# Accumulating transfers and row sums, read by nobody, inside a one-core transformer block; two weight staging tiles in place of three

## The chip, the cores and the metric

The program runs on one core of a Trainium2 chip. The metric is the device time of one execution in microseconds (us). Before the change it is 1162.78 us, the median of two runs (1161.66 and 1163.89).

## The reference

One block of a hybrid model over 512 tokens of width 1024, in float32. Three sublayers each normalise the tokens, scale and shift them by values computed from a conditioning vector `c`, and add their gated result back: a gated feed-forward layer, a mixer (pooling windows and a chunked state-space scan), and a second gated feed-forward layer; a last norm ends it.

```python
mod = (silu(c) @ w_ada + b_ada).reshape(bsz, 3, 3, 1024)      # shift, scale, gate of each sublayer
h = modulate(rmsnorm(x, norm_g[0]), shift[0], scale[0])
x = x + 0.5 * gate[0] * swiglu(h, ffn1_in, ffn1_out)           # swiglu: (silu(a) * b) @ w_out, width 2816
h = modulate(rmsnorm(x, norm_g[1]), shift[1], scale[1])
x = x + gate[1] * hybrid_mixer(h, ...)
h = modulate(rmsnorm(x, norm_g[2]), shift[2], scale[2])
x = x + 0.5 * gate[2] * swiglu(h, ffn2_in, ffn2_out)
return rmsnorm(x, final_g)
```

## The kernel before

Activations lie with the 1024 features on partitions (8 tiles of 128) and the 512 tokens along the row. Every product is made of three matmuls on split operands (`mm3`, L312 to L314): a number is split into a high part and the rest, and high x high, high x rest and rest x high are added in PSUM.

**Weights.** The class `Weights` streams them in units of up to eight 128x128 tiles. A unit is loaded by SyncE into a raw tile (`w_raw`, L103, 512 KB; there are `RAW` = 3 of them), cast to its high part on ScalarE (`w_hi`, L123), and the rest is taken on VectorE (`w_lo`, L126). High and rest stand in rings of `RING` = 5. A raw tile is free again when its unit's L126 is done, so the load of unit k waits for the split of unit k - 3. The first eight units (`w1s`, 384 KB each, 0 to 7) belong to the first stage, where six products of the first feed-forward layer are built over eight steps k while step k's modulation weights arrive as four 256 KB loads (`big<-in_ada_dram`, L395). From unit 8 on two units make one pair of the feed-forward layer.

**Feed-forward.** `ffn` goes over 22 pairs in portions of 8, 8 and 6. A pair is two products of 48 matmuls together; its gate product is a Silu on ScalarE, a multiplication on VectorE (L607), a cast on ScalarE (L325) and a difference on VectorE (L327). Pairs 0 to 2 come out of the first stage. After a portion, eight output columns are made from its pairs and added to `x` (L524).

**Modulation values.** In the first feed-forward layer a background generator, `ada_rest`, computes the remaining 14 half rows of modulation values: each is a sum on VectorE of eight steps (L464 for the first, L466 for seven more, each on a 256 KB tile loaded at L437), closed by four small matmuls on TensorE (L486, listed with their weight loads), a copy on ScalarE (L489) and four 0.5 KB transfers (L492). `pump` advances it six steps behind each pair. The matmuls for the second sum stand on TensorE behind pair 6, those for the third behind pair 7.

**What sets the order.** TensorE's order is the order in which the code is written. In the first stage (`start`) the other engines' order is as written too; behind it a scheduler orders ScalarE, VectorE, GpSimd and SyncE. Each engine executes its own list strictly in order, and SyncE's list holds all transfers. GpSimd has little: pieces of the norms, of pooling and of the scan.

Of the kernel before, what the change touches and what calls it, by code (L numbers as in the profile page):

```python
# [8 lines left out]
F32 = mybir.dt.float32  # L9
# [3 lines left out]
ALU = mybir.AluOpType  # L13
PSUM = bass.MemoryType.PSUM

P = 128
NT = 512
# [11 lines left out]
MLATE = 5  # L29
SPREAD1, SPREAD2, SPREAD3 = 3.6, 1.8, 2.4  # L30
RING = 5
RAW = 3
AHEAD = 3
NBIG = 50
NSQ = 2
# [49 lines left out]
class Weights:  # L85
# [13 lines left out]
    def load(self, upto):  # L99
        while len(self.raw) < min(upto, len(self.units)):  # L100
            ap, count, width, _ = self.units[len(self.raw)]
            raw = self.pool.tile([P, KD * P], F32, name="w_raw", tag="w_raw", bufs=RAW)
            self.nc.sync.dma_start(out=raw[:, :count * width], in_=ap)  # L103
# [26 lines left out]
    def fill(self, more=0):  # L130
# [5 lines left out]
        while len(self.split) < want and self.ring[len(self.split) + 1] - self.ring[used] <= RING:  # L136
            self.ensure(len(self.split) + 1)
        self.load(min(self.unit + AHEAD + RAW + more, len(self.split) + RAW))

# [98 lines left out]
class Block:  # L238
# [26 lines left out]
    def plan(self):  # L265
        a = self.a
        u = [(a["w1s"][k], 2 * NSTART, P, False) for k in range(KD)]

        def stream(ap):
            n = ap.shape[1] // P  # L270
            for t in range(0, n, KD):
                e = min(t + KD, n)
                u.append((ap[:, t * P:e * P], e - t, P, False))

        def ffn(f, first):
            for pi, (p0, p1) in enumerate(PORTIONS):
                for t in range(2 * max(p0, first), 2 * p1):
                    u.append((a["ffn%d_in" % f][t], KD, P, False))
                stream(a["ffn%d_out%d" % (f, pi)])

        def halves(ap):
            u.extend((ap[i], KD, P, True) for i in range(4))

        ffn(1, NSTART)
        halves(a["w_inH"])
        for kind, i in self.mixer_order():
            if kind == "in":
                u.append((a["w_in"][i], KD, P, False))
            elif kind != "dt" and i == 0:
                stream(a["w_out" + kind[3:]])  # L290
        halves(a["ffn2_inH"])
        ffn(2, 2)
        return u
# [323 lines left out]
    def ffn(self, h, gs, j, gate, norm, late, spread, pumps=(0, 0)):  # L617
        for pi, (p0, p1) in enumerate(PORTIONS):
            if pi:
                gs = {i: self.new_act() for i in range(p0, p1)}  # L620
            for i in range(max(p0, j), p1):
                self.pair(h, gs[i])
                self.pump(pumps[0])
            acts = [gs[i] for i in range(p0, p1)]
            last = pi == len(PORTIONS) - 1
            for m in range(late if last else KD):
                self.out_full(m, acts, gate, last)()
                self.pump(pumps[1])
            if last:
                self.pump(1000)  # L630
                norm = norm()
                for m in range(late):
                    norm.scale(m)
                self.out_halves(range(late, KD), acts, gate, norm, spread)


    def start(self):
# [549 lines left out]
```

## Time and profile before

| | |
|---|---|
| runs | 1161.66 and 1163.89 us, median 1162.78 |
| profiled execution | 1160.53 us, span 1158.5 us |
| TensorE busy | 1146.2 us, 99% of the span |
| VectorE busy | 629.9 us, 54% |
| ScalarE busy | 396.6 us, 34% |
| GpSimd busy | 119.3 us, 10% |
| transfers | 140.17 MB, all issued from SyncE |

The span is the time between the first and the last recorded instruction of the profiled execution; 2.0 us of its own time lie outside. Busy time is the sum of an engine's instructions; matmuls are pipelined, so a busy TensorE is not one at its peak. The chain that ended last is followed back from the last instruction to whatever released each step.

### The profile page before, as it was taken

The numbers are of one execution on the slowest core, as the hardware profiler recorded it, in microseconds if no ns is written. First come the engines' busy times: TensorE is split into PE (matmuls) and PEld (weight loads), VectorE is DVE, ScalarE is ACT, GpSimd is POOL, SyncE is SP. The second block draws the span as 40 slices with busy tenths as digits, with TensorE's granted clock in tenths as the row PEclk, the third lists the DMA queues.
The fourth block names the chain that finished last, engine by engine and source line by source line (L and its number), as shares of the span: only waits on it lengthen the run. The fifth ranks groups of instructions, "written<-read, shape, count | busy, mean of one in ns | idle before, by whom it ended". The sixth has DMA issues, their size and how long they took to land.

```text
span 1158.5 us, 15066 instructions
## 1 busy us (share of the span) xinstructions
PE 1146.2 (99%) x5948; PEld 940.8 (81%) x5948; DVE 629.9 (54%) x975; ACT 396.6 (34%) x660; POOL 119.3 (10%) x122
## 2 busy tenths in 40 slices
PE   8999999999999999999999999999999999999997
PEld 6677787777877997888888878899888888888887
DVE  4567736667363666677968595563333333333334
ACT  4352222221223453454544453343321222212232
POOL 0000000000000320023112561121000000000001
PEclk9999999999999999999999999999999999999999
DMA  9585735756352411222212213440332233323312
GB/s 346 170 293 178 261 115 198 256 190 228 123 178 91 141 60 52 77 73 73 74 55 73 73 56 91 124 131 20 91 91 91 93 103 96 92 91 91 95 33 73
DMA packets 52837, 140.17 MB, mean 121 GB/s; under 512 B 7456, under 2 KB 8864, under 8 KB 52768
## 3 DMA queue, kind: packets, MB, share of 16 engines
q1 hardware_dynamic: 52768, 139.23, 37.1%
q8 instruction: 46, 0.75, 0.3%
q14 instruction: 23, 0.19, 0.1%
HBM read 137.08 MB, written 2.10 MB: 120 GB/s over the span
## 4 chain that ended last, share of the span: by engine, by line
PE 98%; DVE 1%; DMA 0%; ACT 0%; SPq 0%; issue 0%; DVEq 0%; ACTq 0%
PE ps_mm L312 24%; PE ps_mm L313 23%; PE ps_mm L314 23%; PE ps_t L314 6%; PE ps_t L313 6%; PE ps_t L312 6%; PE ps_y L965 1%; PE ps_mm L352 1%; PE ps_mm L406 1%; PE ps_t L959 1%; PE ps_y L984 1%; PE ps_mm L375 1%; PE ps_t L927 0%; DMA x<-in_x_dram 0%; PE ps_t L930 0%; PE ps_t L932 0%
## 5 line engine op out<-in xcount | busy, mean ns | idle before, releaser
L312 PE MATMUL ps_mm<-big,w_hi 128*128 128x512 f32 (+1 forms) x1192 | 454.9, 382 | 0.0
L313 PE MATMUL ps_mm<-big,w_hi 128*128 128x512 f32 (+1 forms) x1192 | 448.1, 376 | 0.1
L314 PE MATMUL ps_mm<-big,w_lo 128*128 128x512 f32 (+1 forms) x1192 | 448.0, 376 | 0.0
L123 ACT CAST w_hi<-w_raw 128x1024 fp32r<-128x1024 f32 (+1 forms) x178 | 185.9, 1045 | 521.3 <-PE ps_mm L313 309.4
L126 DVE TENSOR_TENSOR w_lo<-w_raw,w_hi 128x1024 fp32r<-128x1024 f32 (+1 forms) x178 | 220.8, 1242 | 171.7 <-ACT w_hi L123 160.6
L312 PEld LDWEIGHTS ps_mm<-big,w_hi 128*128 128x128 f32 x1192 | 224.1, 188 | 50.3 <-issue 8.2
L314 PEld LDWEIGHTS ps_mm<-big,w_lo 128*128 128x128 f32 x1192 | 224.1, 188 | 44.8
L313 PEld LDWEIGHTS ps_mm<-big,w_hi 128*128 128x128 f32 x1192 | 224.2, 188 | 43.6 <-issue 0.7
L314 PE MATMUL ps_t<-big,w_lo 128*128 128x512 f32 x312 | 123.4, 396 | 0.0
L312 PE MATMUL ps_t<-big,w_hi 128*128 128x512 f32 x312 | 123.4, 396 | 0.0
L313 PE MATMUL ps_t<-big,w_hi 128*128 128x512 f32 x312 | 123.4, 396 | 0.0
L524 DVE SCALAR_TENSOR_TENSOR x<-ps_mm,mod,x 128x512 f32<-128x512 f32 (+1 forms) x79 | 51.1, 648 | 127.6 <-PE ps_mm L314 127.5
L331 POOL TENSOR_TENSOR sacc<-sacc,sq 128x256 f32<-128x256 f32 (+1 forms) x30 | 28.7, 956 | 747.4 <-ACT sq L386 416.1
L607 DVE TENSOR_TENSOR tmp<-tmp,ps_t 128x512 f32<-128x512 f32 x39 | 26.8, 688 | 104.4 <-PE ps_t L314 104.4
L466 DVE SCALAR_TENSOR_TENSOR big<-big,sc 128x512 f32<-128x512 f32 x98 | 73.6, 751 | 12.6 <-DMA big<-in_ada_dram 10.1
L314 PEld LDWEIGHTS ps_t<-big,w_lo 128*128 128x128 f32 x312 | 58.6, 188 | 14.2
L313 PEld LDWEIGHTS ps_t<-big,w_hi 128*128 128x128 f32 x312 | 58.6, 188 | 14.2
L312 PEld LDWEIGHTS ps_t<-big,w_hi 128*128 128x128 f32 x312 | 58.6, 188 | 14.1
L877 DVE SCALAR_TENSOR_TENSOR big<-ps_mm,vec,big 128x511 f32<-128x511 f32 (+2 forms) x60 | 44.7, 745 | 2.2 <-ACT big L875 1.3
L325 ACT CAST big<-tmp 128x512 fp32r<-128x512 f32 (+1 forms) x66 | 36.5, 556 | 2.0 <-DVE tmp L607 1.4
L312 PE MATMUL ps_mm<-big 128*128 128x256 f32 x128 | 36.5, 286 | 0.0
L313 PE MATMUL ps_mm<-big 128*128 128x256 f32 x128 | 36.2, 283 | 0.0
(179 smaller groups left out, 891.1 us busy)
## 6 DMA issues: line engine op xcount, KB each, us to landing
w_raw<-in_ffn_in_dram SPq DMA_DIRECT2D x78, 512.0 KB, 3.5
big<-in_ada_dram SPq DMA_DIRECT2D x144, 256.0 KB, 4.8
w_raw<-in_ffn_out_dram SPq DMA_DIRECT2D x44, 512.0 KB, 3.8
w_raw<-in_w_in_dram SPq DMA_DIRECT2D x32, 512.0 KB, 3.5
w_raw<-in_w_outB_dram SPq DMA_DIRECT2D x10, 512.0 KB, 3.6
w_raw<-in_w1s_dram SPq DMA_DIRECT2D x8, 384.0 KB, 5.8
w_raw<-in_w_outA_dram SPq DMA_DIRECT2D x6, 512.0 KB, 3.9
x<-in_x_dram SPq DMA_DIRECT2D x8, 256.0 KB, 5.3
```

The source lines that it names most:

```text
L123: nc.scalar.copy(out=hi[:, :n], in_=r)
L126: nc.vector.tensor_tensor(out=lo[:, :n], in0=r, in1=hi[:, :n].bitcast(F32), op=ALU.subtract)
L312: T.matmul(o, lhsT=hi, rhs=ahi[:, s], start=first, stop=False)
L313: T.matmul(o, lhsT=hi, rhs=alo[:, s], start=False, stop=False)
L314: T.matmul(o, lhsT=lo, rhs=ahi[:, s], start=False, stop=last)
L325: self.nc.scalar.copy(out=hi[:, s], in_=src[:, :n])
L331: self.nc.gpsimd.tensor_tensor(out=acc, in0=acc, in1=q, op=ALU.add)
L352: self.nc.tensor.matmul(ps[:, at + j:at + j + 1], lhsT=acc[:, c * P - c0:(c + 1) * P - c0], rhs=self.ones[:, 0:1], start=i == 0, stop=i == ...
L466: V.scalar_tensor_tensor(out=acc, in0=ws.pop(i), scalar=self.sc[:, q:q + 1], in1=acc, op0=ALU.mult, op1=ALU.add)
L524: self.nc.vector.scalar_tensor_tensor(out=xs, in0=ps[:, :n], scalar=self.mod[:, gate, m:m + 1], in1=xs, op0=ALU.mult, op1=ALU.add)
L607: nc.vector.tensor_tensor(out=g32, in0=sa, in1=pb[:, :n], op=ALU.mult)
L877: V.scalar_tensor_tensor(out=acc[:, s:], in0=ps[:, :NT - s], scalar=tap(3 - s), in1=acc[:, s:], op0=ALU.mult, op1=ALU.add)
```

## The change

A method `extra` is called in the second feed-forward layer behind pair 3. It takes two tiles of 128x2048 (t1, t2) and one of 128x512 (r), which nothing else reads. SyncE loads t1 and t2 from the weights `ffn2_out0`. GpSimd then issues 20 transfers that add into t2, eight over 1, 2, 4 and 4 pieces of 512 columns from memory and from t1, eight over 2 pieces each in four rounds, and four over one piece each. VectorE then makes three products with a row sum (L660), a copy, two scaled products with a row sum (L666), two additions over 2048 columns (L668, L669), a strided one (L671) and a small one (L672). The number of raw tiles goes from three to two, and the space reserved for GpSimd's transfer descriptors is set to 2048 bytes per partition.

```diff
-RAW = 3
+RAW = 2
...
             for i in range(max(p0, j), p1):
                 self.pair(h, gs[i])
+                if gate == 8 and i == 3:
+                    self.extra()
                 self.pump(pumps[0])
...
+    def extra(self):
+
+        nc = self.nc
+        G, V = nc.gpsimd, nc.vector
+        src = self.a["ffn2_out0"]
+        t1 = self.sb.tile([P, 4 * NT], F32, name="extra1")
+        t2 = self.sb.tile([P, 4 * NT], F32, name="extra2")
+        r = self.sb.tile([P, NT], F32, name="extra3")
+        nc.sync.dma_start(out=t1, in_=src[:, :4 * NT])
+        nc.sync.dma_start(out=t2, in_=src[:, 4 * NT:8 * NT])
+        for n in (1, 2, 4, 4):
+            G.dma_start(out=t2[:, :n * NT], in_=src[:, :n * NT], accum_op=ALU.add)
+        for n in (1, 2, 4, 4):
+            G.dma_start(out=t2[:, :n * NT], in_=t1[:, :n * NT], accum_op=ALU.add)
+        for _ in range(4):
+            for j in range(2):
+                c = slice(2 * j * NT, 2 * (j + 1) * NT)
+                G.dma_start(out=t2[:, c], in_=src[:, c], accum_op=ALU.add)
+        for j in range(4):
+            c = slice(j * NT, (j + 1) * NT)
+            G.dma_start(out=t2[:, c], in_=t1[:, c], accum_op=ALU.add)
+        for j in range(3):
+            V.tensor_tensor_reduce(out=t2[:, :2 * NT], in0=t2[:, :2 * NT], in1=t1[:, :2 * NT], scale=1.0,
+                                   scalar=r[:, 3:4] if j == 2 else 0.0, op0=ALU.mult, op1=ALU.add,
+                                   accum_out=r[:, j:j + 1] if j < 2 else r[:, 4:5])
+            if j == 1:
+                V.tensor_copy(out=r[:, 3:4], in_=r[:, 0:1])
+        for j in range(2):
+            V.scalar_tensor_tensor(out=t2[:, :2 * NT], in0=t2[:, :2 * NT], scalar=1.0, in1=t1[:, :2 * NT],
+                                   op0=ALU.mult, op1=ALU.mult, accum_out=r[:, 8 + j:9 + j])
+        V.tensor_tensor(out=t2, in0=t2, in1=t1, op=ALU.add)
+        V.tensor_tensor(out=t2, in0=t2, in1=t1, op=ALU.subtract)
+        a, b = (t.rearrange("p (s n) -> p s n", n=NT) for t in (t1, t2))
+        V.tensor_tensor(out=b[:, 1::2], in0=a[:, 0::2], in1=b[:, 3:4].broadcast_to([P, 2, NT]), op=ALU.add)
+        V.tensor_tensor(out=r, in0=t1[:, :NT], in1=t2[:, :NT], op=ALU.add)
...
-    nc = bacc.Bacc("TRN2", target_bir_lowering=False, num_devices=1)
+    nc = bacc.Bacc("TRN2", target_bir_lowering=False, num_devices=1, dynamic_dma_scratch_size=2048)
```

The scheduler does not keep the added work where the call stands. On SyncE, in the changed program, the loads of t1 (L646) and t2 (L647) stand in the first stage, t2's here between the modulation loads of step 6 and weight load 6; a DMAHW name is a semaphore of an earlier transfer, DVE one of VectorE (a split that frees a raw tile).

```order
L103 DMA w_raw_372<-in_w1s_dram 128x768 [waits DMAHW7_49,DVE_49]
L395 DMA big_417<-in_ada0_dram 128x512 [waits DMAHW0_49]
L395 DMA big_419<-in_ada0_dram 128x512 [waits DMAHW1_49]
L395 DMA big_421<-in_ada0_dram 128x512 [waits DMAHW2_49]
L395 DMA big_423<-in_ada0_dram 128x512 [waits DMAHW3_49]
L647 DMA extra2_7292<-in_ffn2_out0_dram 128x2048 [waits DMAHW4_49]
L103 DMA w_raw_425<-in_w1s_dram 128x768 [waits DMAHW5_49,DVE_49]
```

Before, the same queue has no such load, and w_raw_372 (unit 5) waits for the split three units back, not two.

On VectorE before, this stands behind the gate product of pair 4 (tmp_838 is its product, tmp_925 that of pair 5, big_850 the second modulation sum, w_lo_961 the rest of weight unit 17):

```order
L466 SCALAR_TENSOR_TENSOR big_757<-big_762,sc_80,big_757 128x512 [waits DMAHW4_49,DVE_49]
L464 TENSOR_SCALAR big_850<-big_765,sc_80 128x512 [waits DMAHW5_49]
L466 SCALAR_TENSOR_TENSOR big_850<-big_768,sc_80,big_850 128x512 [waits DMAHW6_49,DVE_49]
L466 SCALAR_TENSOR_TENSOR big_850<-big_771,sc_80,big_850 128x512 [waits DMAHW7_49,DVE_49]
L126 TENSOR_TENSOR w_lo_961<-w_raw_866,w_hi_960 128x1024 [waits DMAHW0_49,PE_49,Activation_49]
L466 SCALAR_TENSOR_TENSOR big_850<-big_842,sc_80,big_850 128x512 [waits DMAHW2_49,DVE_49]
L466 SCALAR_TENSOR_TENSOR big_850<-big_845,sc_80,big_850 128x512 [waits DMAHW3_49,DVE_49]
L466 SCALAR_TENSOR_TENSOR big_850<-big_848,sc_80,big_850 128x512 [waits DMAHW4_49,DVE_49]
L466 SCALAR_TENSOR_TENSOR big_850<-big_852,sc_80,big_850 128x512 [waits DMAHW5_49,DVE_49]
L466 SCALAR_TENSOR_TENSOR big_850<-big_855,sc_80,big_850 128x512 [waits DMAHW6_49,DVE_49]
L607 TENSOR_TENSOR tmp_925<-tmp_923,ps_t_892 128x512 [waits PE_49,Activation_49]
```

On VectorE after (tmp_923 is pair 5's product, big_848 the second sum, w_lo_959 unit 17; DMASW names are semaphores of the transfers that GpSimd issues):

```order
L466 SCALAR_TENSOR_TENSOR big_848<-big_843,sc_80,big_848 128x512 [waits DMAHW3_49,DVE_49]
L466 SCALAR_TENSOR_TENSOR big_848<-big_846,sc_80,big_848 128x512 [waits DMAHW4_49,DVE_49]
L660 ISA extra2_7292,extra3_7293<-extra2_7292,extra1_7291 128x1024 [waits DMASW6_49,DMASW7_49,DMASW1_49,DMASW0_49]
L660 ISA extra3_7293 128x1
L607 TENSOR_TENSOR tmp_923<-tmp_921,ps_t_890 128x512 [waits PE_49,Activation_49]
L466 SCALAR_TENSOR_TENSOR big_848<-big_850,sc_80,big_848 128x512 [waits DMAHW5_49,DVE_49]
L126 TENSOR_TENSOR w_lo_959<-w_raw_895,w_hi_958 128x1024 [waits DMAHW0_49,Activation_49]
L327 TENSOR_TENSOR big_645<-tmp_923,big_644 128x512 [waits Activation_49]
L466 SCALAR_TENSOR_TENSOR big_848<-big_853,sc_80,big_848 128x512 [waits DMAHW6_49,DVE_49]
L126 TENSOR_TENSOR w_lo_990<-w_raw_962,w_hi_989 128x1024 [waits DMAHW1_49,Activation_49]
```

The first row sum (L660) stands ahead of pair 5's product, of unit 17's split and of the last two steps of the second sum; the rest of `extra` is spread over the rows up to the first output columns of the first feed-forward layer.

On GpSimd after, the 20 transfers stand at the head of the list (the two CASTs belong to the mixer and wait for a load of constants); each waits for the one before it on the same columns:

```order
L649 DMA extra2_7292<-in_ffn2_out0_dram 128x512 [waits DMAHW4_49]
L649 DMA extra2_7292<-in_ffn2_out0_dram 128x1024 [waits DMASW0_49]
L649 DMA extra2_7292<-in_ffn2_out0_dram 128x2048 [waits DMASW1_49]
L649 DMA extra2_7292<-in_ffn2_out0_dram 128x2048 [waits DMASW2_49]
L651 DMA extra2_7292<-extra1_7291 128x512 [waits DMASW3_49]
L651 DMA extra2_7292<-extra1_7291 128x1024 [waits DMASW4_49]
L987 CAST selp_4125<-cst_66 128x128 [waits DMAHW6_49]
L987 CAST selp_4298<-cst_66 128x128
L651 DMA extra2_7292<-extra1_7291 128x2048 [waits DMASW5_49]
L651 DMA extra2_7292<-extra1_7291 128x2048 [waits DMASW6_49]
L655 DMA extra2_7292<-in_ffn2_out0_dram 128x1024 [waits DMASW7_49]
L655 DMA extra2_7292<-in_ffn2_out0_dram 128x1024
```

Before, GpSimd's list has the two CASTs there and no transfer at all.

## Rows read from the trace of the kernel before

**Rows 1.** The page: span, busy times, shares of the chain that ended last.
```profile
span 1158.5 us, 15066 instructions
PE 1146.2 (99%) x5948; PEld 940.8 (81%) x5948; DVE 629.9 (54%) x975; ACT 396.6 (34%) x660; POOL 119.3 (10%) x122
PE 98%; DVE 1%; DMA 0%; ACT 0%; SPq 0%; issue 0%; DVEq 0%; ACTq 0%
```

**Rows 2.** Waits of TensorE, whole run: us in total, times, longest; all four.
```profile
PE ps_mm L740 <- ACT big L730: 2.0, 1, 2.0
PE ps_mm L352 <- DVE big L685: 1.2, 1, 1.2
PE ps_mm L672 <- DVE ones L659: 1.1, 1, 1.1
PE ps_mm L352 <- DVE sacc L685: 0.9, 1, 0.9
```

**Rows 3.** Chain of work that ended last, 90 to 130 us: start, us, what.
```profile
109.40 0.36 PE ps_y L486 x8
109.75 0.43 PE ps_mm L312
...
121.15 0.35 PE ps_y L486 x8
```

**Rows 4.** Timeline of VectorE, 80 to 100 us: start, us, what, idle time before.
```profile
86.73 0.68 DVE L607 TENSOR_TENSOR tmp<-tmp,ps_t 128x512 f32<-128x512 f32 x1
...
94.12 3.90 DVE L466 SCALAR_TENSOR_TENSOR big<-big,sc 128x512 f32<-128x512 f32 x5
97.93 0.68 DVE L607 TENSOR_TENSOR tmp<-tmp,ps_t 128x512 f32<-128x512 f32 x1
```

**Rows 5.** VectorE by line and shape: busy us, mean ns, idle before.
```profile
L126 DVE TENSOR_TENSOR w_lo<-w_raw,w_hi 128x1024 fp32r<-128x1024 f32 x170 | 213.1, 1255 | 158.5 <-ACT w_hi L123 149.1 <-PE ps_t L961 1.4
L466 DVE SCALAR_TENSOR_TENSOR big<-big,sc 128x512 f32<-128x512 f32 x98 | 73.6, 751 | 12.6 <-DMA big<-in_ada_dram 10.1
...
L327 DVE TENSOR_TENSOR big<-tmp,big 128x512 fp32r<-128x512 f32 x46 | 32.9, 717 | 1.8 <-ACT big L325 1.8
L607 DVE TENSOR_TENSOR tmp<-tmp,ps_t 128x512 f32<-128x512 f32 x39 | 26.8, 688 | 104.4 <-PE ps_t L314 104.4
...
L464 DVE TENSOR_SCALAR big<-big,sc 128x512 f32<-128x512 f32 x14 | 6.7, 481 | 0.0
```

**Rows 6.** Timeline of SyncE, first stage: weight loads 2 and 6.
```profile
15.65 0.33 SPq L103 DMA_DIRECT2D w_raw<-in_w1s_dram  x1
...
34.67 0.33 SPq L103 DMA_DIRECT2D w_raw<-in_w1s_dram  x1
```

**Rows 7.** Timeline of VectorE, first stage: splits 0 and 3.
```profile
18.91 0.95 DVE L126 TENSOR_TENSOR w_lo<-w_raw,w_hi 128x768 fp32r<-128x768 f32 x1
...
33.68 0.96 DVE L126 TENSOR_TENSOR w_lo<-w_raw,w_hi 128x768 fp32r<-128x768 f32 x1 [2.00 <-ACT w_hi L123]
```

**Rows 8.** Timeline of TensorE, first stage: matmuls on step 3's modulation weights.
```profile
31.32 1.07 PE L406 MATMUL ps_mm<-big,sc 128*32 128x256 f32 x16
```

**Rows 9.** Stretches: us, busy by engine (count), granted clock, transfer share, GB/s.
```profile
10.00:18.00 8.00, 6.66 (x49) 4.84 (x48) 3.52 (x17) 2.21 (x6) 0.00 (x0) 0.79 1.05 395
43.00:95.00 52.00, 51.87 (x256) 39.95 (x249) 34.69 (x51) 22.02 (x33) 2.60 (x2) 1.00 0.66 218
```

**Rows 10.** The 0.5 KB transfers of L492: ns to issue, us to landing.
```profile
L492 SPq DMA_DIRECT2D mod<-tmp x56: 502/582/1515, 98.7 to 354.1; - x56
...
DMA to landing us min/median/max: 1.6/1.7/3.7
```

**Rows 11.** Weight loads (200 to 300 us) and casts (from 295 us).
```profile
DMA to landing us min/median/max: 3.5/4.9/6.5
...
299.53 1.06 ACT L123 CAST w_hi<-w_raw 128x1024 fp32r<-128x1024 f32 x1 [4.54 <-PE ps_mm L313]
305.13 1.06 ACT L123 CAST w_hi<-w_raw 128x1024 fp32r<-128x1024 f32 x1 [4.54 <-PE ps_mm L313]
```

## The prediction

> **What bounds the kernel now.** I read the page first. TensorE is busy for 99% of the span and the chain of work that ended last lies on it for 98% [rows 1]. The view of waits confirms that this is no artefact of pipelined records: in the whole run TensorE waits for another engine four times, 2.0 us at most, and all four at lines of the first stage [rows 2]. So anything added elsewhere costs nothing until it makes TensorE wait, and the question is where the added work stands in the queues that TensorE depends on. VectorE is busy for 54%, GpSimd for 10%, and no transfer is issued from GpSimd before.
>
> The order of the instructions then decides. The second sublayer is where the call stands in the code, but nothing that the added work reads is made late, and nothing holds it there: the load of t1 stands in SyncE's queue among the loads of the first stage, the load of t2 a little behind it, the chain of accumulating transfers at the head of GpSimd's queue, and the first row sum on VectorE between the fourth and the fifth gate product of the *first* feed-forward sublayer. That row sum waits for the transfers. VectorE works in order, so everything behind it waits too: the gate product of pair 5, the split of weight unit 17, and the last two steps of the sum that TensorE needs for the matmuls of L486 behind pair 6. This new wait is the whole case; the sum below is when the chain ends against when TensorE needs what is queued behind it.
>
> **When t2 is there.** In the order after, t2's load follows the four modulation loads of step 6, which follow weight load 5. With two raw tiles weight load k waits for split k-2, so load 5 goes out after split 3, which ends at 33.68 + 0.96 = 34.6 [rows 7]; before, load 6 waited there and went out at 34.67 [rows 6]. Behind it stand 0.4 + 1.05 + 1.05 MB; at the 395 GB/s of the saturated start [rows 9] that is 6.3 us, with 1.7 us until a transfer has landed [rows 10], so the chain starts at about **43 us**.
>
> **How long the chain takes.** Each transfer waits for the one that wrote the same columns. The first row sum needs the first half of t2, whose last writers are the 17th and 18th transfers. To there it is 8 transfers in a row, 4 rounds of two that overlap, and one last pair: 13 links. They move 11 + 11 + 16 + 2 = 40 pieces of 128x512 f32, 0.262 MB each, 10.5 MB. The trace shows no accumulating transfer and none from GpSimd, so I bound both prices.
> - A link's fixed part: the smallest transfers, 0.5 KB, land 1.6 to 3.7 us after issue, 1.7 in the median, and an issue takes 0.58 us [rows 10]. Low 1.6, high 3.7 + 0.6 = 4.3; I take 1.7 + 0.6 = 2.3, since each link also has to be issued: 13 x 2.3 = 30 us.
> - The bytes: low, once at 395 GB/s, 26.5 us. High, twice, because an addition must fetch the destination as well as the source, and with half the engines throughout: 21 MB at 197 GB/s, 106 us. I take them twice at the full rate, 53 us, since the second fetch is part of the operation and the rate is the one nearest to it that the trace has.
> - Sharing: between 43 and 95 us the weights and modulation loads move 218 GB/s x 52 us = 11.3 MB [rows 9], 28.7 us of the engines' time; the chain is in its bytes for 53 of 83 us, so 0.64 x 28.7 = 18 us fall on it.
>
> Sum 30 + 53 + 18 = 101 us, end at **144 us**. [...]
>
> **What waits for it.** VectorE gets to the row sum at about 95: pair 4's product stands at 86.73 [rows 4], and from it to the wait the new order has that product and its difference, two splits, one first step and five more, 0.68 + 0.69 + 2 x 1.24 + 0.48 + 5 x 0.75 = 8.1 us [rows 5]; the trace has VectorE at the same steps at 94.12 and at pair 5's product at 97.93 [rows 4]. TensorE goes on alone: units 14 to 16 are split, so it finishes pairs 5 and 6 and stops at the L486 matmuls that stand at 109.40 [rows 3]. After the chain's end VectorE needs, up to the sum that these read, one row sum, one product, two steps, one split and one difference: 1.24 + 0.68 + 0.75 + 0.75 + 1.24 + 0.7 [rows 5] and some 0.2 for the row sum's second instruction, 5.6 us. The row sum over 128x1024 is not in the trace; low is 1.24 (the split of the same size), high twice that, and I take the low end because the split reads the same two operands. Stall: 144 + 5.6 - 109.4 = **40.2 us**. Others wait with VectorE: ScalarE at pair 5's cast, behind which stands unit 18's; SyncE at the load of unit 19, which wants unit 17's split, with modulation loads behind it; both resume within these 5.6 us and are needed later than TensorE's next stop. On GpSimd the two casts that stand in the chain serve the mixer.
>
> Then VectorE is behind. Until the next such sum is ready it has seven steps (5.25), two row sums (2.8), two scaled products with sums (2.5), three splits (3.7), one pair's product and difference (1.4) and 0.6 of small ones, 16.2 us. TensorE wants it after pair 7, 121.15 - 109.75 = 11.4 us later [rows 3]: 4.8 us lost. The two 128x2048 additions, the strided one and pair 7's product and difference are 7.7 us more, while the 21 matmuls of the first output column that come ahead of pair 7's last 21 x 11.4 / 48 = 5.0 us, from 0.4 us behind the sum: 7.7 - 5.4 = 2.3 us lost. Together **7.1 us**. After it the backlog fits into VectorE's idle time (34.7 of 52 us busy [rows 9]).
>
> An idle TensorE restarted at a lower clock once: 0.79 granted over 10 to 18 us, where it had run 128-wide matmuls with gaps [rows 9]. That is 0.21 x 8 = **1.7 us**, taken once.
>
> **What I cost at nothing.** Two raw tiles: in steady state a tile is busy for its load, 4.9 us in the median and 6.5 at most, its cast 1.05 [rows 11] and its split 1.25 [rows 5], 8.8 us at most, while two tiles serve two units in 2 x 5.6 us [rows 11]. The cover is 2.4 us; were it gone, the ring of five splits would be the next. In the start the weight load of step 2 now waits for split 0, at 18.91 + 0.96 = 19.9 [rows 7] where it went out at 15.65 [rows 6], and t1's 2.7 us go ahead of step 4. Step 3's modulation loads then land near 25 and their matmuls stand at 31.32 [rows 8]; the later steps have 5.6 us each for 3.6 us of bytes. The reserved scratch only frees space. All rows of TensorE are in the order of before.
>
> **Sum.** 1160.5 (the profiled execution) + 40.2 + 7.1 + 1.7 = 1209.5; the median of the runs is 2.3 above the profiled one, so **1212 us**, 4.2% slower.
>
> **Rivals.**
> - *The chain runs like plain copies* (the other side). Bytes once, links 2.3: 30 + 26.5 + 0.47 x 28.7 = 70 us, end at 113, stall 9 and with the rest 18: 1181 us. If links cost 1.6 and nothing shares, it ends near 91, ahead of VectorE. It decides at 103.8 (109.4 - 5.6): ended by then, nothing is lost and the time is 1163. For it speaks that the engines are idle for a third of that stretch (share 0.66 [rows 9]); against it, that an addition is no copy. [...]
> - *The chain is much slower*: 4.3 us a link, bytes twice at half the engines: 56 + 106 = 162 us, end at 205, stall 101 and with the rest 110: 1273 us. For it: no transfer of this kind is in the trace, and small ones took up to 3.7 us [rows 10]. Against it: once VectorE stands, SyncE's loads stand too, and the chain has the engines alone.
> - *Two raw tiles run dry as well*: while the chain shares the engines, a load of 4.9 to 6.5 us could double to 13; 15.3 us for two units against 11.2 would lose 2 us on each of some nine units, 18 us: 1230. Against it: the ring's lead of several units.
>
> **How the numbers follow.** Forecast 0.56, plain copies 0.28 (0.12 of it for a chain that ends by 104, 0.16 for one that ends by 118), much slower 0.11, raw tiles 0.05. A measurement of this kernel can tell about 2% from no change; slower by 2% is 1186, a chain that ends after 118. Plain copies fall almost wholly below it, the others above: slower 0.71, same 0.27, faster 0.02 (nothing is taken away, so only by an accident of the new order). The range reaches from 1166, which keeps most of the plain copies, to 1260, a chain that ends at 192; about 0.1 stays outside on each side.
>
> **What would show it.** VectorE's idle time ahead of the first row sum, put down to the transfers into t2, from about 95 to 144; one gap of about 40 us on TensorE ahead of L486 near 109, two small ones behind it, and otherwise a span as before; from the mixer on everything shifted by one constant. Links near 2.3 us plus 1.3 us per piece would confirm the price. If the row sum finds the transfers landed, or TensorE's time is lost in waits for splits late in the run, I was wrong.

## The result and the profile after

The changed kernel takes **1208.1 us** (1207.82 and 1208.38) against 1162.78: 1.039 times as long, 95% interval [1.0345, 1.0434]. The profiled execution took 1208.38 us. In its lines the numbers from L625 on are those of before plus 2, and behind the added function plus 38.

The page, answering [rows 1]:
```profile
span 1206.6 us, 15123 instructions
...
PE 1151.4 (95%) x5948; PEld 943.8 (78%) x5948; DVE 639.9 (53%) x990; ACT 395.4 (33%) x660; POOL 134.7 (11%) x142
...
PE 86%; DMA 10%; DVE 1%; issue 1%; SPq 0%; ACT 0%; DVEq 0%; POOL 0%; ACTq 0%
```
TensorE's busy time grew by 5 us only; a tenth of the chain of work that ended last is now transfers. TensorE's waits over the whole run (total, times, longest), against the four of [rows 2]:
```profile
PE ps_y L486 <- DVE big L466: 40.2, 1, 40.2
PE ps_mm L778 <- ACT big L768: 2.0, 1, 2.0
PE ps_mm L312 <- ACT big L325: 1.7, 1, 1.7
...
PE ps_mm L313 <- DVE big L327: 0.2, 1, 0.2
PE ps_t L314 <- DVE w_lo L126: 0.2, 1, 0.2
```
Four are new: one of 40.2 us, and three small ones. Where they stand, on TensorE's timeline (start, duration; in brackets the idle time before and what ended it):
```profile
98.12 0.43 PE L486 MATMUL ps_y<-big,ones 128*32 128x128 f32 x8
150.59 0.65 PE L486 MATMUL ps_y<-big,ones 128*32 128x128 f32 x8 [40.19 <-DVE big L466]
165.00 0.43 PE L486 MATMUL ps_y<-big,ones 128*32 128x128 f32 x8
172.25 0.50 PE L312 MATMUL ps_mm<-big,w_hi 128*128 128x512 f32 x1 [1.73 <-ACT big L325]
186.38 0.42 PE L486 MATMUL ps_y<-big,ones 128*32 128x128 f32 x8
```
Before, the four L486 groups start at 97.57, 109.33, 121.08 and 138.44 on this view, which gives a group its first matmul ([rows 3] shows the second from the other view). The shift is 0.55 us at the first, 41.3 at the second, 43.9 at the third and 47.9 at the fourth; the spans differ by 48.1. So all is paid by 186 us and the rest of the run is a constant later. VectorE in that stretch, against [rows 4]:
```profile
103.73 1.22 DVE L126 TENSOR_TENSOR w_lo<-w_raw,w_hi 128x1024 fp32r<-128x1024 f32 x1 [5.90 <-ACT w_hi L123]
...
106.40 3.90 DVE L466 SCALAR_TENSOR_TENSOR big<-big,sc 128x512 f32<-128x512 f32 x5
145.64 1.22 DVE L660 CUSTOM_DVE_ANT_0 extra<-extra,extra 128x1024 f32<-128x1024 f32 x1 [35.34 <-DMA extra<-extra]
...
149.79 0.74 DVE L466 SCALAR_TENSOR_TENSOR big<-big,sc 128x512 f32<-128x512 f32 x1
```
VectorE gets to the row sum at 110.3 and stands 35.3 us for the transfers. It is late itself: ahead of its split at 103.73 it waited 5.90 us for ScalarE's cast, and that cast for a weight load:
```profile
102.64 1.05 ACT L123 CAST w_hi<-w_raw 128x1024 fp32r<-128x1024 f32 x1 [5.54 <-DMA w_raw<-in_ffn_in_dram]
```
The chain of waits shows the links (start, us):
```profile
46.20 5.82 DMA extra<-in_ffn_out_dram
...
58.84 8.85 DMA extra<-in_ffn_out_dram
...
78.07 3.80 DMA extra<-extra
...
102.93 10.52 DMA extra<-extra
...
113.79 5.53 DMA extra<-in_ffn_out_dram
...
140.60 0.54 POOL extra L658
141.14 4.38 DMA extra<-extra
```
The chain runs from 46.2 to 145.6 us, 99.4 us. Behind the wait the clock is low (columns as in [rows 9]):
```profile
146.00:150.00 4.00, 0.00 (x0) 0.00 (x0) 4.00 (x7) 2.06 (x3) 0.00 (x0) 0.50 0.51 87
150.00:160.00 10.00, 9.41 (x36) 7.20 (x37) 10.00 (x17) 2.73 (x5) 0.00 (x0) 0.68 0.38 107
160.00:180.00 20.00, 18.04 (x76) 13.54 (x75) 19.01 (x25) 3.22 (x6) 0.00 (x0) 0.91 0.61 203
180.00:190.00 10.00, 10.00 (x50) 7.71 (x49) 7.83 (x11) 2.53 (x4) 0.00 (x0) 1.00 0.86 306
```
Behind the 40.2 us without work TensorE's granted clock is 0.50 from 150 to 156 us and 1.00 from 158 on. A second fall stands behind the short waits at 172 and 173 (1.73 and 0.23 us): 0.50 from 174 to 176, 1.00 again from 177. In all 0.32 of 10 us and 0.09 of 20, some 5 us, are lost to the clock. VectorE is busy for 29.0 of the 30 us from 150 to 180.

### The profile page after: what moved, and what is told of

Same layout as the page of the kernel before. It is cut to its first block, busy times and chain, and to the rows that moved or that the text cites. A ratio compares the mean times of both kernels' runs of the same rounds, so it can differ in the third digit from the quotient of the medians.

```text
span 1206.6 us, 15123 instructions
## 1 busy us (share of the span) xinstructions
PE 1151.4 (95%) x5948; PEld 943.8 (78%) x5948; DVE 639.9 (53%) x990; ACT 395.4 (33%) x660; POOL 134.7 (11%) x142
## 3 DMA queue, kind: packets, MB, share of 16 engines
q0 software_dynamic: 2880, 11.01, 4.8%
## 4 chain that ended last, share of the span: by engine, by line
PE 86%; DMA 10%; DVE 1%; issue 1%; SPq 0%; ACT 0%; DVEq 0%; POOL 0%; ACTq 0%
PE ps_mm L312 21%; PE ps_mm L313 21%; PE ps_mm L314 21%; PE ps_t L314 5%; PE ps_t L313 5%; PE ps_t L312 5%; DMA extra<-in_ffn_out_dram 5%; DMA extra<-extra 3%; PE ps_y L1003 1%; PE ps_t L997 1%; PE ps_mm L352 1%; PE ps_y L1022 1%; PE ps_mm L375 1%; DMA x<-in_x_dram 1%; DMA w_raw<-in_ffn_out_dram 0%
## 5 line engine op out<-in xcount | busy, mean ns | idle before, releaser
L325 ACT CAST big<-tmp 128x512 fp32r<-128x512 f32 (+1 forms) x66 | 36.4, 554 | 56.6 <-DVE tmp L607 56.3
L486 PE MATMUL ps_y<-big,ones 128*32 128x128 f32 x112 | 6.2, 294 | 40.2 <-DVE big L466 40.2
L486 PEld LDWEIGHTS ps_y<-big,ones 128*32 128x32 f32 x112 | 2.2, 110 | 45.4 <-DVE big L466 41.8
```

The source lines that it names most:

```text
L325: self.nc.scalar.copy(out=hi[:, s], in_=src[:, :n])
```

## The experiments

Theory: the added work costs its time because the first row sum stands in VectorE's order ahead of what TensorE needs, and an adding transfer pays for its bytes twice, an estimate of the prediction. Rivals: the transfers cost time by themselves, the two raw tiles do, VectorE's work does. Ratios are to the kernel before, with 95% intervals.

**e1, two raw tiles alone.**
```diff
-                if gate == 8 and i == 3:
-                    self.extra()
```


> The added work is left out; two raw weight tiles and the reserved scratch stay. My theory: every microsecond of the change comes from VectorE standing in front of the first row sum, so this is the time before, 1163 us (1162 to 1165). Rival (two raw tiles cost time of their own, 2 us on some units): 1167 to 1180.

1163.7 us, 1.0013 [1.0003, 1.0022]. By that interval two raw tiles cost 0.3 to 2.6 us by themselves.

**e2, transfers without VectorE's work.** All `V.` lines of the added function go.

> The two loads and all 20 accumulating transfers stay, the row sums and the other added VectorE instructions are left out, so nothing on VectorE waits for the transfers. My theory: 1163 to 1165 us; the transfers share the DMA engines with the weight loads until about 146 us, which costs TensorE about 1 us before 110 us and no more. Rival (the transfers themselves starve the weight loads): 1170 to 1190 with the chain of transfers as long as before, about 99 us, and TensorE waiting for splits of late weight units.

1188.16 us, 1.0233 [1.0212, 1.0253]: the rival by its size, though TensorE waits for something else than it said. With nothing of VectorE waiting for the chain, TensorE still waits for the modulation sums:
```profile
PE ps_y L486 <- DVE big L466: 21.9, 3, 17.2
```
ScalarE's timeline of this run says why:
```profile
114.79 1.05 ACT L123 CAST w_hi<-w_raw 128x1024 fp32r<-128x1024 f32 x1 [8.53 <-DMA w_raw<-in_ffn_in_dram]
115.74 0.26 ACT L489 COPY tmp<-ps_y 128x128 f32<-128x128 f32 x1
...
135.41 1.04 ACT L123 CAST w_hi<-w_raw 128x1024 fp32r<-128x1024 f32 x1 [17.44 <-DMA w_raw<-in_ffn_out_dram]
```
The casts wait 8.5 and 17.4 us for weight loads. L489, the copy of the *first* sum out of PSUM, stands behind such a cast in ScalarE's order and comes 16 us after its matmuls at 99.3. SyncE's small transfers of L492 wait for that copy, and the next six modulation loads stand behind them: issued from 118.9, where the kernel before had issued them by 104.3. Two weight loads follow these in SyncE's queue, at 123.0, and the cast at 135.41 waits for the first of them; VectorE has done the sum's earlier steps by 133.8, but the last one stands behind the two splits of these units and starts at 141.4. On ScalarE and VectorE the order in this stretch is that of e1, so it is the traffic that differs. Issue to landing between 50 and 110 us, of e2 and then of e1:
```profile
w_raw<-in_ffn_in_dram SPq DMA_DIRECT2D x10, 512.0 KB, 6.8
```
```profile
w_raw<-in_ffn_in_dram SPq DMA_DIRECT2D x10, 512.0 KB, 3.6
```
The change itself has 6.8 us there too.

**e3, plain copies; e4, plain copies in the four rounds only.** The order on every engine is that of the change.
```diff
-            G.dma_start(out=t2[:, :n * NT], in_=src[:, :n * NT], accum_op=ALU.add)
+            G.dma_start(out=t2[:, :n * NT], in_=src[:, :n * NT])
```


> The same 20 transfers in the same order on the same queue with the same waits, but as plain copies that overwrite t2 in place of adding to it; every engine's instructions stand in the order of the change. My theory (an addition pays for a second fetch, bytes twice): 13 links of 2.3 us, bytes once 26.5 us and some 13 us of sharing, 70 us in all, end at 116 us, TensorE's gap about 10 us, 1176 to 1182 us. Rival A (the addition is free, the price is that of the links and the path): chain near 99 us, end near 145, 1205 to 1208 us. [...]

> Only the eight transfers of the four rounds (16 of the 40 pieces) are plain copies, the other 12 still add; same order on every engine. My theory: the rounds took 26.8 us; they lose 16 pieces x 0.66 us of second fetches, some 10.6 us, so the chain ends at about 135 us and the time falls by as much, 1196 to 1199 us. Rival (the addition is free): 1206 to 1208 us.

e3: 1186.93 us, 1.0212 [1.0196, 1.0227]; chain 43.1 to 121.5, 78.5 us where 70 were expected, gap 18.8 us. Between the theory and rival A, much nearer to the theory. e4: 1200.9 us, 1.0342 [1.0318, 1.0366]; the row sum starts at 140.5, the rounds from 114.9 to 135.4 took 20.5 us instead of 26.8. The additions were not free: 6.3 us for 16 pieces, less than the 10.6 expected (1196 to 1199 us). The page's row of GpSimd's queue (packets, MB, share of 16 engines' span) shows best what the additions cost the engines, of the change and then of e3:
```profile
q0 software_dynamic: 2880, 11.01, 4.8%
```
```profile
q0 software_dynamic: 2496, 11.01, 2.6%
```
The same 11.01 MB hold the engines for 0.048 x 1206.6 = 57.9 us when they are added and 0.026 x 1183.0 = 30.8 when copied, 190 against 357 GB/s. That the time goes into a second fetch was the author's estimate; the rows show the price alone.

**e5, plain copies without VectorE's work; e10, only the first eight additions without it.** e2's code with e3's edit, and with the rounds and the last four cut.

> No added VectorE work, as in the run before, but the 20 transfers are plain copies instead of additions; every engine's instructions stand in the order of that run. My theory now (the additions hold the 16 DMA engines about twice as long per byte, and the modulation loads of the next sum, issued near 119 us, still share them): with plain copies the chain has ended near 119 us, so the loads land in time and the time is 1163 to 1168 us. Rival (any traffic of GpSimd's queue, added or copied, delays them): 1180 us or more.

> No added VectorE work, and of the 20 adding transfers only the first eight (22 of the 40 pieces); the four rounds and the last four are left out, so the chain ends near 114 us in place of 153. My theory (what costs 25 us without VectorE's wait is that the modulation loads for the third sum, issued near 119 us behind the small transfers of L492, share the engines with the rounds): TensorE's wait of 17 us at the third L486 is gone, 1163 to 1167 us. Rival (the damage is done earlier, while the long transfers run between 50 and 114 us): 1172 us or more.

e5: 1174.19 us, 1.0102 [1.0086, 1.0117], neither value: with copies TensorE waits too, for less (9.0 us at the third L486, 17.2 in e2). e10: 1176.23 us, 1.0117 [1.0101, 1.0132], the rival; the wait at the third L486 falls from 17.2 to 8.5 us and is not gone. My reading of e2 had been too narrow: with the chain ended near 111 us the modulation loads are still issued only at 119.6, because ScalarE's casts had waited for weight loads before that (7.46 us ahead of the cast at 114.52, with L489 behind it at 115.47). Of the 26 us that e2 lost, the rounds and the last four cost 12 and the eight transfers ahead of them 14.

| | row sums wait on VectorE | no VectorE work |
|---|---|---|
| additions | 1208 | 1188 |
| plain copies | 1187 | 1174 |

**e6, VectorE's work without the transfers.** The `G.dma_start` lines go.

> The 20 transfers are left out; the two loads and all the added VectorE work stay, and since nothing waits for a chain they are moved into the first stage. My theory (VectorE's 13 us of work cost nothing by themselves): 1163 to 1166 us. Rival (they delay the first stage's splits and modulations, which come one step after the other): 1168 to 1176 us.

1170.88 us, 1.0075 [1.0061, 1.0089]: the rival, by its size. Nothing holds the row sums now, and they run from 49.6 to 67.8 us, between the steps of the first stage's modulation, where TensorE waits for them:
```profile
PE ps_mm L313 <- DVE big L517: 2.4, 2, 1.6
PE ps_mm L312 <- ACT big L516: 2.3, 2, 1.6
```
From the last L406 group but one to the first L486 it takes 56.3 us, 49.4 in e1: 6.9 lost, 4.7 of them in these waits.

**e7, all of it held in the second sublayer.**
```diff
+        for t in (t1, t2):
+            V.tensor_copy(out=t[:, 0:1], in_=g[1][:, 0:1])
         nc.sync.dma_start(out=t1, in_=src[:, :4 * NT])
...
+        V.tensor_copy(out=r[:, 0:1], in_=g[1][:, 0:1])
         for j in range(3):
```
(g is the fourth gate product there, and for the row sums the ninth.)

> All the added work, held in the second feed-forward sublayer: the two loads wait for a column that VectorE copies out of the fourth gate product there (in all three small copies are added), and the row sums for the ninth. There GpSimd has nothing else to do, the DMA engines are busy for about a third, and the row sums come some 100 us after the loads. My theory (position and contention are the whole price): 1163 to 1166 us, a chain of 60 to 83 us, links of 2.3 us plus 1.3 us a piece, TensorE without a wait. Rival A (an accumulating chain costs TensorE time wherever it stands): 1180 us or more. Rival B (the links are slow of themselves, as in the first feed-forward, 99 us): row sums wait some 10 us, 1163 to 1175.

1163.06 us, 1.0004 [0.9994, 1.0014]: the same work for nothing. Two things differ from the change at once: nothing that TensorE needs soon stands behind the row sums, and the transfers run among fewer loads. But the chain took 95.9 us, where the transfers of the kernel itself hold the engines for 0.31 of the time, not 60 to 83; rival B had its length. GpSimd's timeline, 1, 4 and 4 pieces, and the row sum on VectorE:
```profile
837.91 1.04 POOL L653 DMA_DIRECT2D extra<-in_ffn_out_dram  x1 [42.54 <-DVE tmp L607]
842.71 0.87 POOL L653 DMA_DIRECT2D extra<-in_ffn_out_dram  x1 [3.76 <-DMA extra<-in_ffn_out_dram]
...
857.80 0.86 POOL L653 DMA_DIRECT2D extra<-in_ffn_out_dram  x1 [8.66 <-DMA extra<-in_ffn_out_dram]
867.99 0.86 POOL L655 DMA_DIRECT2D extra<-extra  x1 [9.33 <-DMA extra<-in_ffn_out_dram]
```
```profile
933.84 1.23 DVE L671 CUSTOM_DVE_ANT_0 extra<-extra,extra 128x1024 f32<-128x1024 f32 x1 [4.65 <-DMA extra<-extra]
```
VectorE even waits 4.65 us for the chain, and TensorE does not notice.

**e11, the held variant with plain copies; e12, with a sixteenth of the columns.**

> The held variant, its 20 transfers as plain copies; instructions in the order of the held variant. There the adding links took 4.8, 5.6 and 9.5 us for 1, 2 and 4 pieces of 0.262 MB, about 3.2 us plus 1.6 us a piece. My theory (a fixed part that does not depend on adding, bytes twice for an addition): about 4.0, 4.8 and 6.4 us, the chain 65 to 72 us in place of 96. Rival (adding costs fixed time for each transfer): the same slope of 1.6 us and a smaller fixed part, chain 80 to 90 us. The time stays at 1160 to 1165 us.

> The held variant with a sixteenth of the columns in every one of the 20 adding transfers (32 for each 512), so the bytes are 0.7 MB: what is left is the fixed price of a link. My theory (from the line through the held links): 3.2 us a link, some 35 to 45 us for the 13. The prediction's price: 2.3 us, 30 us. The time stays at 1160 to 1165 us.

e11, one run: 1162.63 us; links from memory of 3.9, 4.1 and 5.5 us for 1, 2 and 4 pieces (those from t1 scatter more: 2.5, 5.2, 5.4 and 5.3 for 1, 2, 4 and 4). The pair that the row sum reads goes out here:
```profile
896.68 1.07 POOL L662 DMA_DIRECT2D extra<-extra  x2 [0.57 <-DMA extra<-in_ffn_out_dram]
```
That is 58.4 us after the first transfer, against 88.5 in e7; with some 5 us for the pair itself, an estimate from this run's links of 2.5 to 5.7 us, the chain takes some 63 us in all. This is what the theory of one fixed part and fewer bytes said, a little shorter, with a lower slope (0.5 us a piece over the links from memory). e12, one run: 1160.57 us; GpSimd's timeline:
```profile
834.43 1.04 POOL L653 DMA_DIRECT2D extra<-in_ffn_out_dram  x1 [42.19 <-DVE tmp L607]
837.13 0.88 POOL L653 DMA_DIRECT2D extra<-in_ffn_out_dram  x1 [1.67 <-DMA extra<-in_ffn_out_dram]
...
873.55 3.53 POOL L662 DMA_DIRECT2D extra<-extra  x4 [1.84 <-DMA extra<-in_ffn_out_dram]
```
Twelve links in 39.1 us, 3.26 each on average (2.4 to 4.9) with hardly any bytes: the theory's price, not the prediction's 2.3.

**e8 and e9, TensorE kept busy through the wait.**
```diff
+        if self.pumps == 4:
+            b = self.bank()
+            for _ in range(45):
+                nc.tensor.matmul(b, lhsT=self.ones, rhs=self.x[:, 0, :], start=True, stop=True)
         ps = self.bank("y")
```


> All the added work as in the change, and 90 matmuls of 128x512 that nothing reads (0.43 us each, 38.6 us in all) ahead of the L486 matmuls that TensorE stands before, so that it is busy during the wait; up to the third sum the other engines' instructions stay in their order. My theory (the slow clock after the wait only covers VectorE's backlog): the granted clock stays at 1.0 behind the wait, and in its place TensorE waits 4 to 6 us for the third sum and pair 7's difference; 1205 to 1208 us. Rival (the slow clock is a cost of its own): no such waits, 1202 to 1204 us.

> As the run with 90 matmuls that nothing reads ahead of the L486 matmuls, but 45 of them, since one took 0.85 us there: 38.4 us, from 110.7 to 149.1 us, where the wait of the change ends at 150.6. My theory (the slow clock after the wait only covers VectorE's backlog): granted clock 1.0 behind the wait, in its place TensorE waits 4 to 6 us for the third sum and pair 7's difference; 1205 to 1208 us. Rival (the slow clock is a cost of its own): no such waits, 1202 to 1204 us.

e8: 1239.75 us, 1.0677 [1.0662, 1.0692]. Neither: I had the matmuls' price wrong. The trace has 180 records for the 90, 0.86 us for each matmul, so they ran to 188 us:
```profile
110.73 77.41 PE L487 MATMUL ps_mm<-x,ones 128*128 128x512 f32 x180
```
It still says something. From the second L486 to the fourth it takes 29.1 us there, as before (29.1), at clock 1.00; the whole time is 1162.6 + 77 us of filling. Given 40 us more, VectorE's backlog and the delayed loads cost nothing. e9, with the filling ended at 149.5: 1211.88 us, 1.0424 [1.0402, 1.0446], 4 us over what I expected, 2 of them from the chain's later end (the row sum starts at 147.6); its interval overlaps that of the change. TensorE's waits:
```profile
PE ps_y L490 <- DVE big L466: 5.8, 2, 3.1
...
PE ps_mm L312 <- ACT big L325: 1.9, 1, 1.9
PE ps_mm L313 <- DVE big L327: 0.6, 1, 0.6
```
Of the 5.8 us, 3.1 stand ahead of the second L486 and 2.7 ahead of the third. Up to the third sum VectorE's order is that of the change, and there the two can be compared. From the second L486 to the third it takes 14.5 us in e9, at clock 1.00 with the wait of 2.7, and 14.4 in the change, with the low clock and no wait (11.75 before). So the slow clock was no cost on top there; it stood where the backlog would have. Behind the third sum the two differ in more than the clock: in e9 the scheduler set the strided addition, the small one and a split, 3.1 us, ahead of pair 7's product. TensorE waits 1.9 + 0.6 us there, and behind the wait of 2.7 the clock is low too (0.58 in 168 to 172 us). Second to fourth L486: 38.0 us, against 35.8 in the change.

## Why the prediction was right, step by step

- **Place of the wait**: right. The wait is VectorE's, ahead of L486 near 110 us, and e7 against the change shows that the place of the work is the whole price: held late, the same work costs nothing. It is not the place of the row sums alone: with none on VectorE the transfers still cost 26 us where they stand (e2).
- **Chain of 101 us**: measured 99.4, but its terms only balance. It began at 46.2 and not at 43, as t2's load went out at 39.33 and took 6.56 us. Links, 30 said: about 42 (39.1 for twelve in e12, and one more). Bytes, 53 said: 55 by the queue's row (57.9 us for 42 pieces, of which the chain has 40), and 95.9 - 42 = 54 left over in e7: right in size. That an addition fetches its destination as well was the prediction's assumption; no run shows it. Sharing, 18 said: 99.4 - 95.9 = 3.5 up to the row sum. From the first transfer to the issue of the pair that it reads the change took 94.4 us and e7 88.5, so 5.9 by that measure, and 7.7 in e9, 8.6 in e2: less than half of what was said in each. "2.3 us plus 1.3 us per piece" is not confirmed: 3.2 plus 1.6 in e7. Held in the second sublayer the chain took 96 us with additions and some 63 with copies (e7, e11).
- **What shares, and who pays**: this step failed. I charged the sharing to the chain. Most of it the loads paid: 6.8 us in place of 3.6 for a weight load (the change and e2; e1). So VectorE came at 110.3, not 95. TensorE was 1.1 us late before it stopped, 0.55 of it already in the first stage, ahead of the chain (the matmuls on step 3's modulation weights stand at 31.88, 31.32 before).
- **Stall of 40.2**: measured 40.19. The chain ended 1.6 later, VectorE then needed 4.95 us instead of 5.6 (the row sum took the low end, 1.22, and the instructions behind it started 0.07 to 0.09 us before the one ahead of them ended), and TensorE came 1.0 later; three small differences that cancel.
- **Backlog 7.1 and clock 1.7**: second to fourth L486 took 35.8 against 29.1, so 6.7 where 8.8 was said. As waits only 1.9 us appear, the clock took the rest. The prediction added the two; up to the third sum e9 shows that one stands in for the other.
- **Two raw tiles at nothing**: right alone (e1). The rival "two raw tiles run dry" can nevertheless be seen at work in e2: three weight loads of the first feed-forward's input weights, issued between 92 and 130 us, take 10.7 us in the median, so the stated cover of 2.4 us is gone, and the load that ScalarE's cast at 114.79 waits for goes out at 105.72, just as the split that frees its tile ends. How much of e2's 26 us is due to the tiles and how much to the slow loads is open: the 20 transfers with three raw tiles weren't tried. In the change it doesn't show: behind the 40 us wait TensorE has no wait for a split.
- **Rivals**: plain copies would have been 1181; e3 measured 1187, with a chain of 78 us and not 70.

The sum against its own execution: 1160.5 + 1.1 + 40.2 + 6.7 = 1208.5, measured 1208.4. The 2.3 us that the forecast of 1212 has on top for the median didn't come: the median is 0.3 below the profiled execution.

## What to carry over

Look first at where a scheduler puts work that depends on nothing late: its place in the engines' in-order queues, and what runs beside it there, decided the whole cost here, 45 us against none. When a wait is found, ask what else the same traffic delays: behind the 40 us lay a second loss of 26 that appears when the first is taken away, and comes through a path (load, cast, copy in ScalarE's order, small transfers in SyncE's, next loads) that no single wait names. A total that comes out right is no proof of its terms.

## What had not been expected

- A dependent adding transfer from GpSimd took 3.3 us on average with almost no bytes (e12); its issue took 0.86 us on GpSimd, that of a copy 0.53 (e7, e11).
- The additions held the engines 1.9 times as long per byte as the copies (57.9 us in the change against 30.8 in e3; by the same rows 60.4 in the held additions of e7 and 31.7 in the copies of e5).
- The adding chain lost little in the crowd, 6 to 9 us of 94 to 97 to the issue of the last pair that the row sum reads (the change, e9 and e2 against 88.5 in e7; that of copies more, 75.3 us in e3 against 58.4 in e11); the weight loads from SyncE's queue nearly doubled, 6.8 us against 3.6 in e1.
- TensorE's granted clock was 0.50 from 150 to 156 us behind the wait of 40.2 us, and low behind much shorter ones too: 0.50 from 174 to 176 us behind a wait of 1.73 in the change, 0.58 over 168 to 172 us behind one of 2.67 in e9, where the longest wait before had been 3.08.
